# Seven block products in a second feed-forward, and modulation steps shared with ScalarE and GpSimd

## The chip, the cores and the metric

The kernel runs on one core of one Trainium2 chip. The metric is device time in microseconds of one execution, as the median of a few runs. The engines go by short names in the profile: PE is TensorE's matmul queue (PEld its weight loads), DVE is VectorE, ACT is ScalarE, POOL is GpSimd, and SP is the queue that issues nearly all DMAs.

## What is computed

Two layers of a transformer block on 256 image tokens (x) and 256 context tokens (ctx) of 1024 channels. Each layer has a feed-forward, a token mix (attention and pooling) and a second feed-forward. Ahead of each stands a norm with a shift and a scale, behind each a gate; these nine vectors per layer come from one conditioning vector per stream, which is the *modulation*.

```python
def mod_vectors(cvec, w_mod, b_mod):
    m = jax.nn.silu(cvec) @ w_mod + b_mod
    return jnp.split(m, N_MOD, axis=-1)

def sandwich_ffn(x, w_gate_up, w_down, g_pre, g_post, shift, scale, gate):
    h = modulate(rms_norm(x, g_pre), shift, scale)
    return x + 0.5 * gate * rms_norm(swiglu(h, w_gate_up, w_down), g_post)

for l in range(DEPTH):
    x = sandwich_ffn(x, ...); ctx = sandwich_ffn(ctx, ...)
    out_x, out_c = token_mix(...)
    x = sandwich_ffn(x + ..., ...)
    if not last: ctx = sandwich_ffn(ctx + ..., ...)
```

All inputs are float32. D_FF is 2816, so there are 22 blocks of 128 hidden channels, each with a gate and an up half. The last feed-forward of the second layer has only x.

## The kernel before

**Precision.** A float32 matmul is made of three faster ones. Every operand is split into a high part, which ScalarE rounds (`split`, line 570), and a low part, the difference, which VectorE subtracts. `mm3` (565) multiplies high by high, high by low and low by high. So each weight that is loaded costs ScalarE one rounding and VectorE one subtraction of two SBUF tensors before TensorE can use it.

**A feed-forward** (`ffn`, 930). For each of the 22 blocks: load the weights, split them (`Stream.prep`, 480, one block ahead), multiply the gate and up halves for all 512 tokens into two PSUM banks (names pg and pu), take silu and product, split again (g). After a group of blocks the down projection of that group follows (name pd), and its result is added up in y. The first blocks (START or LEAD, 2 or 3) are done for half of the tokens at a time, so that TensorE can begin while the other half is still being normed. With the last down projections the tokens are *closed* one tile of 128 after the other (`close`, 860): squares, the power -0.5 on GpSimd (`power`, 744, name rs_st), gate, residual, norm for the next stage, transposes on TensorE (pt), shift and scale, and the split into the next stage's input h.

**Seven products.** For the pair in `SEVEN`, here only the second layer's first feed-forward (1, 0), a block is not computed as eight products of quarter size but as seven, in Strassen's manner (`gate_up_seven`, 974; name p_ps): 84 matmuls of 256 columns instead of 48 of 512. For this GpSimd forms sums of the weights (`prep_seven`, 493; name s_wk), four additions of 128x512 per block, and once per feed-forward sums of the tokens (`Input.add_up`, 778), eight more, all of which are split as well. VectorE adds the partial products. The groups are then five of four to six blocks (`S_GROUPS`) instead of three (`F_GROUPS`). The tokens must be laid out in pairs, in the order 2, 0, 3, 1; the stage before has to close them in that order (`NEXT_SEVEN`, `ORDER`, `PAIRED`).

**Modulation** (`mod_steps`, 669). One vector takes nine steps. Eight load 512 KB of w_mod each (name wm) and multiply it by one scalar per partition, adding into an accumulator (acc) of 128x1024 for each of the two streams: a `tensor_scalar` for the first, a `scalar_tensor_tensor` for the others, both on VectorE. From the gate of the second layer's token mix on there is only one stream. The ninth step folds the accumulators: sixteen DMAs of 64 KB, three GpSimd additions per stream (part), a small matmul (pm). The first two vectors of layer 0 are made in another way at the start; the other sixteen, 144 steps, are a queue `todo`. After each block of a feed-forward `fill(rate)` (715) records so many steps of it: `RATE` in the first feed-forward (0, 0), 2.6 steps per block, `LATER` in (0, 1), 2.6, 4.2 and 5.6 in its groups, `NONE` in (1, 0).

**The order of the work.** Nothing is issued as it is written. `Recorder` takes every operation with a rank (its place in the program) and a price by engine and size (`price`, 216; a GpSimd addition is 0.155 us plus 2.09 ns per element of a partition, and each engine is priced for itself). `Recorder.order` (301) then plays the program through: at each step it takes the operation that can start first, by data, by its engine's clock and by a free place, and among equals the one of lowest rank. A `margin` lets an operation count as ready that much later, a `haste` earlier. The result is one fixed order per engine, which the chip follows with semaphores. All lines of the profile are therefore L384, where the operations are issued, and groups are told apart by the names of the tiles. Tiles live in numbered places: sixteen "big" ones for weights, h, g and y, ten "wk" ones of 4 KB per partition for wm, acc, part, tt, the sums and the closings, two for raw weights, eight PSUM banks.

Of the kernel before, what the change touches and what calls it, by code (L numbers as in the profile page):

```python
# [28 lines left out]
S_GROUPS = ((0, 4), (4, 8), (8, 12), (12, 16), (16, 22))  # L29
SEVEN = {(1, 0)}  # L30
NEXT_SEVEN = {(1, 0)}
ORDER = (2, 0, 3, 1)
# [7 lines left out]
LIMITS = {"ps": 1}  # L40
RATE = (2.6, 2.6, 2.6)
LATER = (2.6, 4.2, 5.6)
NONE = (0.0,) * 5
# [141 lines left out]
class Recorder:  # L185
# [9 lines left out]
    def __init__(self, places, limits):  # L195
        self.places, self.limits = places, limits
        self.ops = []
        self.seq = {}
        self.delay = 0
        self.margin = 0.0  # L200
        self.haste = 0.0
        for e in self.ENGINES:
            setattr(self, e, _Engine(self, e))
# [35 lines left out]
    def record(self, engine, method, args, kw):  # L239
# [16 lines left out]
        for v, target in [(v, False) for v in ins] + [(v, True) for v in outs]:  # L256
# [19 lines left out]
            keep.append((op, p0, p1, bits, writes))  # L276
            buf.log = keep
        op.after = after
        op.waits = len(after)
# [122 lines left out]
def tile_dit_block(  # L402
# [56 lines left out]
    class Stream:  # L459
        def __init__(self):  # L460
            self.plan = []
            self.ready = []
            self.raws = []
            self.taken = 0
            self.ahead = AHEAD
            self.sevens = 0

# [25 lines left out]
        def prep_seven(self, raw):  # L493

            (a11, a12), (a21, a22) = ((raw[:, i, 0:512], raw[:, i, 512:D]) for i in range(2))
            s12, s34 = wtile([P, 2, 512], "s12"), wtile([P, 2, 512], "s34")
            rec.margin = 0.0 if self.sevens else 2 * MARGIN
            self.sevens += 1
            nc.gpsimd.tensor_add(s12[:, 0, :], a21, a22)
            rec.margin = 0.0  # L500
            nc.gpsimd.tensor_sub(s12[:, 1, :], s12[:, 0, :], a11)
# [140 lines left out]
    def first_mod(j):  # L642
# [24 lines left out]
        rec.haste = 0.0  # L667

    def mod_steps(l, j):
        acc = [None, None]  # L670
        streams = (0,) if l == DEPTH - 1 and j >= 5 else (0, 1)
        for k in range(KD):
            def step(k=k):
                wm = wtile([P, D], "wm")
                nc.sync.dma_start(out=wm, in_=wmod[l, j, k])
                for v in streams:
                    if k == 0:
                        acc[v] = wtile([P, D], "acc")
                        nc.vector.tensor_scalar(
                            out=acc[v], in0=wm, scalar1=csil[:, k, v : v + 1], scalar2=None, op0=ALU.mult  # L680
                        )
                    else:
                        nc.vector.scalar_tensor_tensor(
                            out=acc[v], in0=wm, scalar=csil[:, k, v : v + 1], in1=acc[v], op0=ALU.mult, op1=ALU.add
                        )
# [26 lines left out]

    debt = [0.0]

    def fill(n):
# [40 lines left out]
    class Input:  # L756
# [3 lines left out]
        def __init__(self, paired):  # L760
# [5 lines left out]
            self.full = {}  # L766
            self.sums = None

        def __getitem__(self, b):
# [8 lines left out]
        def add_up(self):  # L778
# [3 lines left out]
            for o in range(2):  # L782
                one, two = self.full[ORDER[o]], self.full[ORDER[2 + o]]
                rec.margin = MARGIN
                a, b, c, d = one[:, lower, :], two[:, lower, :], two[:, upper, :], one[:, upper, :]
                nc.gpsimd.tensor_sub(a, b, a)
                rec.margin = 0.0
                nc.gpsimd.tensor_sub(b, c, b)
# [7 lines left out]
    def new_h(paired=False):  # L796
        return Input(paired)
# [13 lines left out]
    def normed(t, l, jshift, n, hf, Hn, sq):  # L811
# [16 lines left out]
        if Hn.paired:  # L828
            Hn.full[t] = hf

    def first_unit(t):
# [252 lines left out]
    def token_mix(l, nxt):  # L1084
# [249 lines left out]

        toks = (2, 3, 0, 1) if full else (0, 1)
        load_gate(l, 5, (0, 1) if full else (0,))
# [13 lines left out]
        for t in toks:  # L1350
# [4 lines left out]
            if Hn is None:  # L1355
                Hn = new_h()
            close(t, pd[t], None, False, nxt, Hn)
# [22 lines left out]

    ffn(0, 0, True, (0, 3), RATE, START, (CS, XS))
    token_mix(0, (0, 6))
    ffn(0, 1, True, (1, 0), LATER, LEAD, (CS, XS))
    ffn(1, 0, True, (1, 3), NONE, LEAD, (0, 1))
    token_mix(1, (1, 6))
# [107 lines left out]
```

## Time and profile before

| | us |
|---|---|
| median of 3 runs | 1662.52 |
| lowest and highest | 1661.26, 1665.65 |
| the profiled execution's own time | 1662.74 |
| its span, from the first to the last instruction | 1661.0 |
| TensorE busy in the span | 1615.6 |
| VectorE, ScalarE, GpSimd busy | 1211.8, 736.4, 355.7 |

By the timeline the first feed-forward begins about 40 us into the span and ends about 412, the first token mix ends about 604, the second feed-forward goes to about 980, the third to about 1334, the second token mix and the last feed-forward to the end. A group of the profile gives line, engine, operation, tiles written and read, shapes, the count, the busy time, the mean of one in ns, and the idle time of the engine ahead of it with what ended it. "Releaser" is inferred from semaphores. Buffer numbers are left out of the names, so w_big is any weight in a big place.

### The profile page before, as it was taken

Reading aid. Unit: us, or ns where it says so; the run is one execution under the profiler, and the core shown is the slowest. Engines: PE = TensorE matmul, PEld = TensorE weight load, DVE = VectorE, ACT = ScalarE, POOL = GpSimd, SP = SyncE. Lnnn points to the kernel's source line nnn. Section 1 sums busy time; section 2 is a strip of 40 time slices with the busy share of each in tenths; the row PEclk is TensorE's granted clock in tenths of the full one; section 3 lists DMA queues with packets and bytes.
Section 4 is the critical chain, followed back from the end, with each engine's and each line's share of the span. In section 5 each row is a group of like instructions: output and inputs, shape, how many; then the busy total and the mean of one; then the engine's idle time right before and its main releaser. Section 6 shows DMA issues by size and latency. Waiting matters only on the chain.

```text
span 1661.0 us, 23503 instructions
## 1 busy us (share of the span) xinstructions
PE 1615.6 (97%) x9074; PEld 1392.5 (84%) x9074; DVE 1211.8 (73%) x1662; ACT 736.4 (44%) x1292; POOL 355.7 (21%) x348
## 2 busy tenths in 40 slices
PE   6999999999999999999999989999999999899998
PEld 5988888888888788888888879989989888779997
DVE  7995766546789779867786588677788688975554
ACT  7522322225566563222222364434434567774442
POOL 1022011101132311110211045363454122210000
PEclk9999999999999999999999999999999999999999
DMA  9466556522221435666698413223233422355551
GB/s 376 185 229 247 203 193 224 183 108 83 89 75 65 160 115 212 237 202 229 217 344 306 150 47 106 77 102 128 77 108 122 143 77 82 128 202 194 201 196 58
DMA packets 98958, 269.09 MB, mean 162 GB/s; under 512 B 9424, under 2 KB 39328, under 8 KB 87072
## 3 DMA queue, kind: packets, MB, share of 16 engines
q1 hardware_dynamic: 98848, 267.60, 45.6%
q8 instruction: 71, 1.16, 0.3%
q14 instruction: 39, 0.32, 0.1%
HBM read 251.80 MB, written 1.09 MB: 152 GB/s over the span
## 4 chain that ended last, share of the span: by engine, by line
PE 85%; DVE 6%; ACT 5%; POOL 2%; issue 1%; DMA 1%; SPq 0%; DVEq 0%; POOLq 0%; ACTq 0%
PE pd_ps L384 26%; PE pg_ps L384 19%; PE pu_ps L384 19%; PE p_ps L384 11%; PE pv_ps L384 2%; PE pk_ps L384 2%; ACT n_wk L384 2%; POOL rs_st L384 2%; PE pq_ps L384 1%; DVE w_big L384 1%; DMA w_big<-in_wmod_dram 1%; PE pt_ps L384 1%; PE po_ps L384 1%; PE pp_ps L384 1%; ACT sx_wk L384 1%
## 5 line engine op out<-in xcount | busy, mean ns | idle before, releaser
L384 DVE TENSOR_TENSOR w_big<-raw_raw,w_big 128x1024 fp32r<-128x1024 f32 x293 | 371.2, 1282 | 124.1 <-ACT w_big L384 123.6
L384 PE MATMUL pd_ps<-w_big,g_big 128*128 128x512 f32 x1848 | 431.5, 394 | 0.0
L384 PEld LDWEIGHTS pd_ps<-w_big,g_big 128*128 128x128 f32 x1848 | 345.8, 188 | 78.4 <-ACT grows L384 0.2
L384 ACT ACTIVATE w_big<-raw_raw 128x1024 fp32r<-128x1024 f32 x293 | 302.8, 1053 | 231.7 <-DMA raw_raw<-in_wgu_dram 103.6
L384 PE MATMUL pu_ps<-h_big,w_big 128*128 128x512 f32 (+1 forms) x1944 | 366.5, 341 | 0.0
L384 PEld LDWEIGHTS pu_ps<-h_big,w_big 128*128 128x128 f32 x1944 | 303.7, 188 | 42.3
L384 PE MATMUL pg_ps<-h_big,w_big 128*128 128x512 f32 (+1 forms) x1752 | 331.8, 344 | 3.8 <-DVE h_big L384 2.4
L384 PEld LDWEIGHTS pg_ps<-h_big,w_big 128*128 128x128 f32 x1752 | 277.1, 191 | 44.1 <-DVE h_big L384 2.9
L384 DVE SCALAR_TENSOR_TENSOR acc_wk<-wm_wk,csil,acc_wk 128x1024 f32<-128x1024 f32 x196 | 245.2, 1290 | 78.8 <-DMA wm_wk<-in_wmod_dram 78.5
L384 POOL TENSOR_TENSOR part_wk<-part_wk 128x512 f32<-128x512 f32 (+2 forms) x84 | 89.0, 1060 | 495.6 <-DMA part_wk<-acc_wk 466.6
L384 ACT ACTIVATE g_big<-tt_wk 128x512 fp32r<-128x512 f32 (+1 forms) x84 | 49.2, 586 | 273.2 <-DVE tt_wk L384 257.2
L384 POOL TENSOR_SCALAR rs_st<-sq_st 128x1 f32<-128x1 f32 x24 | 7.6, 316 | 448.0 <-ACT n_wk L384 447.9
L384 POOL TENSOR_TENSOR s_wk<-raw_raw 128x512 f32<-128x512 f32 x38 | 63.8, 1687 | 131.6 <-DMA raw_raw<-in_wgu_dram 94.2
L384 PE MATMUL p_ps<-h_big,w_big 128*128 128x256 f32 x684 | 86.9, 281 | 0.0
L384 PEld LDWEIGHTS p_ps<-h_big,w_big 128*128 128x128 f32 x684 | 83.7, 189 | 0.3
L384 PE MATMUL p_ps<-ht_big,w_big 128*128 128x256 f32 x684 | 83.3, 280 | 0.0
L384 PEld LDWEIGHTS p_ps<-ht_big,w_big 128*128 128x128 f32 x684 | 81.6, 189 | 0.0
L384 DVE TENSOR_TENSOR g_big<-tt_wk,g_big 128x512 fp32r<-128x512 f32 (+1 forms) x84 | 57.8, 688 | 29.9 <-ACT g_big L384 29.9
L384 PE MATMUL pd_ps<-w_big,mix_big 128*128 128x512 f32 x288 | 71.9, 399 | 0.5 <-DVE mix_big L384 0.5
L384 ACT ACTIVATE tt_wk<-pg_ps 128x512 f32<-128x512 f32 (+1 forms) x67 | 35.8, 534 | 75.3 <-PE pg_ps L384 62.4
L384 DVE TENSOR_TENSOR y_big<-y_big,pd_ps 128x512 f32<-128x512 f32 x72 | 47.9, 683 | 27.9 <-PE pd_ps L384 27.8
L384 DVE TENSOR_TENSOR w_big<-s_wk,w_big 128x1024 fp32r<-128x1024 f32 x38 | 55.8, 1468 | 16.5 <-ACT w_big L384 16.4
(157 smaller groups left out, 1769.6 us busy)
## 6 DMA issues: line engine op xcount, KB each, us to landing
raw_raw<-in_wgu_dram SPq DMA_DIRECT2D x84, 1024.0 KB, 4.9
wm_wk<-in_wmod_dram SPq DMA_DIRECT2D x128, 512.0 KB, 6.9
raw_raw<-in_wdn_dram SPq DMA_DIRECT2D x44, 1024.0 KB, 5.2
part_wk<-acc_wk SPq DMA_DIRECT2D x224, 64.0 KB, 2.4
raw_raw<-in_wkq_dram SPq DMA_DIRECT2D x8, 1024.0 KB, 4.8
raw_raw<-in_wout_dram SPq DMA_DIRECT2D x8, 1024.0 KB, 4.9
w_big<-in_wmod_dram SPq DMA_DIRECT2D x7, 1024.0 KB, 15.0
gb_wk<-grow SPq DMA_DIRECT2D x10, 512.0 KB, 7.1
```

The lines of the kernel that those rows point to most:

```text
L384: getattr(getattr(nc, op.engine), op.method)(*[self.real(a) for a in op.args], **{k: self.real(a) for k, a in op.kw.items()})
```

## The change

- `SEVEN` gets (0, 1) as well: the first layer's second feed-forward, the second of four, uses seven products in its blocks 3 to 21, five groups, and halves by paired tokens.
- For this the first token mix closes its tokens in the order 2, 0, 3, 1 and keeps their normed values for the token sums.
- The steps of the modulation are spread anew: 3.6, 4.4 and 4.8 per block in the first feed-forward (93 in place of 57), 1.2 in the second, 1.3 in the third.
- While the first feed-forward is recorded (`helps`), the second stream of a step is made by a ScalarE product into a tile of its own ("pr", a wk place) and a GpSimd addition of 128x1024; the first of a vector is written into the accumulator directly. Afterwards both streams are VectorE's again.
- The margins of 6 and 12 us ahead of the first GpSimd sums are replaced by `hold`: in the planner's order, the first weight sum of each block and the first token sum come after the last operation of the last closing (`Input.done`).

```diff
-SEVEN = {(1, 0)}
-NEXT_SEVEN = {(1, 0)}
+SEVEN = {(0, 1), (1, 0)}
+NEXT_SEVEN = {(0, 6), (1, 0)}
...
-RATE = (2.6, 2.6, 2.6)
-LATER = (2.6, 4.2, 5.6)
+RATE = (3.6, 4.4, 4.8)
+LATER = (1.2,) * 5
+LAST = (1.3,) * 5
...
+        if self.hold is not None:
+            after.setdefault(self.hold, False)
         op.after = after
...
-            rec.margin = 0.0 if self.sevens else 2 * MARGIN
-            self.sevens += 1
+            rec.hold = H["now"].done
             nc.gpsimd.tensor_add(s12[:, 0, :], a21, a22)
-            rec.margin = 0.0
+            rec.hold = None
...
+                    c = csil[:, k, v : v + 1]
                     if k == 0:
                         acc[v] = wtile([P, D], "acc")
-                        nc.vector.tensor_scalar(
-                            out=acc[v], in0=wm, scalar1=csil[:, k, v : v + 1], scalar2=None, op0=ALU.mult
-                        )
+                    if v and helps[0]:
+                        o = acc[v] if k == 0 else wtile([P, D], "pr")
+                        nc.scalar.activation(o, wm, AF.Copy, scale=c)
+                        if k:
+                            nc.gpsimd.tensor_add(acc[v], acc[v], o)
+                    elif k == 0:
+                        nc.vector.tensor_scalar(out=acc[v], in0=wm, scalar1=c, scalar2=None, op0=ALU.mult)
                     else:
                         nc.vector.scalar_tensor_tensor(
-                            out=acc[v], in0=wm, scalar=csil[:, k, v : v + 1], in1=acc[v], op0=ALU.mult, op1=ALU.add
+                            out=acc[v], in0=wm, scalar=c, in1=acc[v], op0=ALU.mult, op1=ALU.add
                         )
...
-                rec.margin = MARGIN
+                rec.hold = self.done
                 a, b, c, d = one[:, lower, :], two[:, lower, :], two[:, upper, :], one[:, upper, :]
                 nc.gpsimd.tensor_sub(a, b, a)
-                rec.margin = 0.0
+                rec.hold = None
...
             Hn.full[t] = hf
+            Hn.done = rec.ops[-1]
...
-        toks = (2, 3, 0, 1) if full else (0, 1)
+        paired = nxt in NEXT_SEVEN
+        toks = (ORDER if paired else (2, 3, 0, 1)) if full else (0, 1)
...
-                Hn = new_h()
+                Hn = new_h(paired)
...
     ffn(0, 0, True, (0, 3), RATE, START, (CS, XS))
+    helps[0] = False
     token_mix(0, (0, 6))
-    ffn(0, 1, True, (1, 0), LATER, LEAD, (CS, XS))
-    ffn(1, 0, True, (1, 3), NONE, LEAD, (0, 1))
+    ffn(0, 1, True, (1, 0), LATER, LEAD, (0, 1))
+    ffn(1, 0, True, (1, 3), LAST, LEAD, (0, 1))
```

More of the change, by code (lines that the diff above doesn't have):

```diff
@@ L199, in __init__ @@
         self.delay = 0
+        self.hold = None
         self.margin = 0.0
@@ L465, in __init__ @@
             self.ahead = AHEAD
-            self.sevens = 0
         def add(self, src, parts, seven=False):
@@ L667, in first_mod @@
         rec.haste = 0.0
+    helps = [False]
     def mod_steps(l, j):
@@ L713, in tile_dit_block @@
     debt = [0.0]
+    helps[0] = True
     def fill(n):
@@ L767, in __init__ @@
             self.sums = None
+            self.done = None
         def __getitem__(self, b):
```

## The prediction

> **What bounds the kernel now.** I read the page first, for the share of each engine and the chain that ended last.
>
> ```profile
> span 1661.0 us, 23503 instructions
> PE 1615.6 (97%) x9074; PEld 1392.5 (84%) x9074; DVE 1211.8 (73%) x1662; ACT 736.4 (44%) x1292; POOL 355.7 (21%) x348
> PE 85%; DVE 6%; ACT 5%; POOL 2%; issue 1%; DMA 1%; SPq 0%; DVEq 0%; POOLq 0%; ACTq 0%
> ```
>
> TensorE (PE) is busy 97% of the span and makes 85% of the chain. An edit pays here if it takes matmuls away, and costs if it makes TensorE wait. So the next view is the table by stretches, cut at the stages that the edit touches: the first feed-forward (40 to 394), the second (613 to 944), the handover to the third (961 to 1022) and the third, which already uses seven block products (1022 to 1299). Columns: length, then busy time and instructions of PE, PEld, DVE, ACT and POOL, granted clock, DMA share, GB/s.
>
> ```profile
> 40.00:394.00 354.00, 354.00 (x1643) 293.04 (x1642) 240.72 (x256) 108.23 (x148) 38.68 (x38) 1.00 0.56 195
> 613.00:944.00 331.00, 330.98 (x1571) 275.13 (x1570) 252.06 (x254) 93.23 (x122) 51.60 (x48) 1.00 0.67 238
> 961.00:1022.00 61.00, 56.15 (x394) 51.96 (x394) 54.35 (x72) 39.41 (x81) 28.67 (x28) 0.97 0.11 38
> 1022.00:1299.00 277.00, 277.00 (x1982) 260.17 (x1981) 211.20 (x228) 116.30 (x153) 126.73 (x72) 1.00 0.31 108
> ```
>
> In all three feed-forwards TensorE has no gap, at full clock: DVE, ACT and POOL hide behind it completely. 4.85 us are idle in the handover. Nothing in these stages can be gained but matmul time; everything else is a question of whether the cover still holds.
>
> **The change part by part.** *Seven products.* The chain in order of time (start, length, what, count) has a plain block of the second feed-forward and the third feed-forward's groups of four blocks.
>
> ```profile
> 898.99 5.55 PE pg_ps L384 x24
> 904.54 5.52 PE pu_ps L384 x24
> ...
> 1054.14 39.60 PE p_ps L384 x336
> 1093.74 22.26 PE pd_ps L384 x96
> 1116.00 39.37 PE p_ps L384 x336
> 1155.37 22.17 PE pd_ps L384 x96
> 1177.54 39.70 PE p_ps L384 x336
> ```
>
> A plain block takes 5.55 + 5.52 = 11.07 us. Four seven-product blocks take 39.60, 39.37 and 39.70, so one takes 118.67 / 12 = 9.89. The first three blocks (LEAD) stay plain halves in both forms, so 19 blocks save 1.18 each: **22.4 us** off the path. The down projections have the same matmuls in five groups instead of three: nothing on TensorE; the extra accumulations on DVE lie under 22 us of TensorE per group.
>
> The groups of DVE in the first feed-forward, 40 to 394, before (count, busy us, mean ns, idle), price its operations:
>
> ```profile
> L384 DVE SCALAR_TENSOR_TENSOR acc_wk<-wm_wk,csil,acc_wk 128x1024 f32<-128x1024 f32 x88 | 110.0, 1289 | 26.7 <-DMA wm_wk<-in_wmod_dram 26.7
> L384 DVE TENSOR_TENSOR w_big<-raw_raw,w_big 128x1024 fp32r<-128x1024 f32 x68 | 84.0, 1255 | 34.7 <-ACT w_big L384 34.7
> L384 DVE TENSOR_TENSOR g_big<-tt_wk,g_big 128x512 fp32r<-128x512 f32 x22 | 15.4, 702 | 7.9 <-ACT g_big L384 7.9
> ...
> L384 DVE TENSOR_SCALAR acc_wk<-wm_wk,csil 128x1024 f32<-128x1024 f32 x14 | 10.1, 749 | 15.2 <-DMA wm_wk<-in_wmod_dram 15.2
> ```
>
> *What the second feed-forward needs from DVE.* In the third one, without modulation, DVE is busy 211.20 of 277. LATER puts 1.2 steps behind each block there, 26 in all, about 16 with two streams. A two-stream step averages (2 x 7 x 1.29 + 2 x 0.75) / 9 = 2.2 us, from these rows, a one-stream step half: 35 + 11 = 46 us, together 257 of 277, 93%. It fits as an average, but within a group of four blocks DVE runs behind and must recover under the 22 us down projection. I book **2 us** of TensorE waiting, with 0 and 15 as ends. LAST gives the third feed-forward 25 one-stream steps, 27 us: 238 of 277, hidden.
>
> *What moves into the first feed-forward.* RATE goes from 57 steps to 92: ten whole vectors and two steps, 82 products per stream, of which 11 start an accumulator, so 71 second-stream additions of 128x1024 go to POOL and 82 products to ACT. The groups of POOL and one of ACT in the same stretch:
>
> ```profile
> L384 POOL TENSOR_TENSOR part_wk<-part_wk 128x512 f32<-128x512 f32 x12 | 18.1, 1507 | 226.7 <-DMA part_wk<-acc_wk 226.2 <-issue 0.4
> L384 POOL TENSOR_TENSOR part_wk<-part_wk 128x256 f32<-128x256 f32 x12 | 10.6, 881 | 0.9
> L384 POOL TENSOR_TENSOR part_wk<-part_wk 128x128 f32<-128x128 f32 x12 | 8.8, 732 | 0.9
> ```
>
> ```profile
> L384 ACT ACTIVATE w_big<-raw_raw 128x1024 fp32r<-128x1024 f32 x68 | 70.1, 1053 | 81.4 <-DMA raw_raw<-in_wgu_dram 41.9 <-PE pd_ps L384 18.1 <-DMA raw_raw<-in_wdn_dram 8.9
> ```
>
> ACT: 82 x 1.05 = 86 us on top of 108, of 354: hidden. DVE: one stream less, 82 instead of 102 operations, so about 25 us less. DMA: 31 more 512 KB loads and four more vectors of sixteen 64 KB pieces are some 20 MB, 56 GB/s on 195, a share of about 0.72; the trace carried 0.95 without a TensorE gap:
>
> ```profile
> 831.00:876.00 45.00, 45.00 (x198) 36.63 (x197) 35.86 (x36) 11.28 (x12) 6.25 (x5) 1.00 0.95 329
> ```
>
> The waits that are new: a POOL addition waits for ACT's product, and an ACT product waits for a free wk place, which a POOL addition gives back. Behind it on ACT stand the roundings of the next weights, and behind a late addition on POOL the rs_st powers of the closings, for which TensorE's transposes wait. So the price hangs on POOL. No 128x1024 addition is in the trace. In the timelines of POOL and of DVE alone:
>
> ```profile
> 489.00 1.17 POOL L384 TENSOR_TENSOR dd_wk<-U_wk 128x591 f32<-128x591 f32 x1 [5.04 <-ACT U_wk L384]
> 490.25 1.17 POOL L384 TENSOR_TENSOR dd_wk<-dd_wk 128x589 f32<-128x589 f32 x1
> 491.49 2.86 POOL L384 TENSOR_TENSOR dd_wk<-dd_wk,U_wk 128x256 f32<-128x256 f32 x4
> ```
>
> ```profile
> 1091.87 2.28 POOL L384 TENSOR_TENSOR s_wk<-s_wk,raw_raw 128x512 f32<-128x512 f32 x1
> ...
> 1103.65 1.29 POOL L384 TENSOR_TENSOR s_wk<-raw_raw 128x512 f32<-128x512 f32 x1
> ```
>
> ```profile
> 1087.82 1.23 DVE L384 TENSOR_TENSOR w_big<-raw_raw,w_big 128x1024 fp32r<-128x1024 f32 x1 [0.40 <-ACT w_big L384]
> ...
> 1090.68 2.31 DVE L384 TENSOR_TENSOR w_big<-raw_raw,w_big 128x1024 fp32r<-128x1024 f32 x1
> ...
> 1102.88 1.39 DVE L384 TENSOR_TENSOR y_big<-y_big,pd_ps 128x512 f32<-128x512 f32 x2 [0.34 <-PE pd_ps L384]
> ```
>
> Alone, a 512-wide addition takes 1.29 us, a 256-wide one 2.86 / 4 = 0.72, a 591-wide one 1.17. So 1024 costs between 1024/591 x 1.17 = 2.0 and 1.29 + 2 x 0.57 = 2.4. And they are not alone: the addition that overlaps DVE's weight subtraction takes 2.28 instead of 1.29, and the subtraction 2.31 instead of 1.23. Each waited out the other. The accumulation that reads PSUM (two in 1.39) disturbed nobody, and the addition beside it took 1.29. So DVE's operations on two SBUF tensors and POOL's additions go one after the other, and the two engines' queues must fit into one stretch of time. A DVE operation holds POOL up for 2.28 - 1.29 = 1.0 us, a 512-wide addition holds DVE up for 1.1, some 0.2 less than it lasts; so 1.8 to 2.2 for 1024.
>
> The common stretch, of 354 us: weight subtractions 68 x 1.0 = 68, g 22 x 0.5 = 11, first stream 71 x 1.0 + 11 x 0.55 = 77, partition sums 20 x (1.1 + 0.5 + 0.3) = 38, additions 71 x 1.8 to 2.2 = 128 to 156. Total 322 to 350, 91 to 99%; before, with 88 + 14 accumulations and 12 sums, 68 + 11 + 96 + 23 = 198, 56%. The planner's prices know POOL and DVE singly and not this, so its order has no room for it. I take the middle, 336, and 92% of the time in use where both queue: 365, **11 us** over the 354. Ends: 0 (the low price, packed) and 43 (350 at 88%).
>
> *The hold.* It replaces a margin by a true predecessor in the planner's order: block sums on POOL come behind the last closing. Before, they ran into it. DVE in the handover, POOL's group of such sums on the page, one of them in the handover, then TensorE:
>
> ```profile
> 973.93 1.50 DVE L384 TENSOR_SCALAR n_wk<-x,rs_st 128x512 f32<-128x512 f32 x1 [0.45 <-POOL rs_st L384]
> ...
> 980.15 3.45 DVE L384 TENSOR_TENSOR h_big<-yg_wk,h_big 128x512 fp32r<-128x512 f32 x2
> ```
>
> ```profile
> L384 POOL TENSOR_TENSOR s_wk<-raw_raw 128x512 f32<-128x512 f32 x38 | 63.8, 1687 | 131.6 <-DMA raw_raw<-in_wgu_dram 94.2 <-DVE c_wk L384 30.4 <-DVE w_big L384 6.6
> ```
>
> ```profile
> 973.87 1.27 POOL L384 TENSOR_TENSOR s_wk<-raw_raw 128x512 f32<-128x512 f32 x1
> ```
>
> ```profile
> 983.66 4.51 PE L384 MATMUL pg_ps<-h_big,w_big 128*128 128x256 f32 x23 [2.42 <-DVE h_big L384]
> ```
>
> Two subtractions of 512 took 3.45, and TensorE waited 2.42 for them. That wait goes: **-2.5 us** of the 4.85. What is late next is the sums themselves, four additions and eight for the tokens, 12 x 1.69 = 20 us behind the last closing; the three lead blocks give 3 x 11.07 = 33 us of cover. Ends: -4.85 and +3. The handover into the second feed-forward gets the same twelve additions anew: **+1**, ends 0 and +4; the other token order there moves no matmul.
>
> **The sum**, against the profiled execution's own 1662.74 us (the span of 1661.0 and 1.7 around it; the median of the three is 1662.52): 1662.7 - 22.4 + 2 + 11 - 2.5 + 1 = 1651.8, so **1652**.
>
> **The rivals.** *POOL and DVE saturate (slower).* With the high price and less than perfect order, the common stretch doesn't fit and the first feed-forward is stretched. ACT stands at a product without a place, the weights behind it are late, and the backlog ends in front of rs_st in the closings. At 350 us and 88% that is 43 us: 1662.7 - 22.4 + 2 + 43 - 2.5 + 1 = 1684. It decides from 21 us on, that is where the common stretch with its gaps exceeds 375. For it: 2.28 and 2.31. Against it: the third feed-forward shows both engines queueing with no gap in TensorE, and the last steps may slip behind the closings. The Trainium skill, SBUF — State Buffer, section "SBUF: two separate sides", has it as a rule: the pair of ports that VectorE and GpSimd share is an exclusive lock, held by one instruction to its end; the rows above agree, 2.28 for 1.29. The Trainium skill, GPSIMD Engine Reference, section "Elementwise — side-by-side cycle accounting", gives 4497 ns for an addition of 2048; half of it, 2.25 as an estimate, would make the sum 71 x 2.05 + 194 = 340.
>
> *DVE is the bound in the second feed-forward.* For a seven-product group at 93% of DVE on average, a backlog of a few us per group on the two-stream part would give 15 us instead of 2: with the rest as forecast 1665, no change. Against it: nothing waited at 76%.
>
> *All is hidden.* The steps fit in (low price): 0 and 0 for the 11 and the 2 and the full 4.85 of the handover give 1662.7 - 22.4 - 4.9 + 1 = 1636.
>
> **How the numbers follow.** 0.3% is 5 us, about what a measurement of this kernel tells from no change. Faster, from the whole gain to a stretch of some 16 us: 0.50. Within 5 us, the forecast's own high end or DVE late in the second feed-forward: 0.15. Slower, by saturation: 0.35. The range leaves out the last us of the hidden case and the worst of saturation: 1637 to 1690; the likeliest case's own is 1637 to 1657.
>
> **What would show it.** Right: the p_ps groups with twice their matmuls, 9.9 us a block; pg_ps and pu_ps fewer; POOL additions of 128x1024 about 71, their mean well over 2.4 (2.8 to 3.4) because they wait for DVE; DVE's acc operations in the first stage likewise; TensorE's gap of 2.42 behind h_big gone. Wrong: TensorE idle over 25 us in the first feed-forward, with ACT waiting for POOL or TensorE waiting for w_big; gaps in TensorE between blocks in the second one with DVE as releaser; an addition near 1.3 us, or additions that leave DVE alone.

## The result and the profile after

| | before | after |
|---|---|---|
| median, us | 1663.47 (1661.26 to 1665.65, 4 runs) | 1769.24 (1768.11 to 1770.55, 4 runs) |
| ratio, 95% interval | | 1.0641, 1.0625 to 1.0657 |
| span of the profiled execution, us | 1661.0 | 1766.3 |

The change makes the kernel 6.4% slower; forecast was 1652, in a range of 1637 to 1690. The page of after, its first line on the span, the engines' busy time, the clock row of the forty slices and the shares of the chain that ended last:

```profile
span 1766.3 us, 25533 instructions
PE 1624.5 (92%) x9758; PEld 1427.7 (81%) x9758; DVE 1395.3 (79%) x1718; ACT 861.6 (49%) x1439; POOL 735.0 (42%) x503
PEclk9988998899799999999999999999999999999999
PE 42%; DVE 23%; DMA 10%; ACT 7%; issue 7%; SPq 6%; POOL 5%; POOLq 0%; DVEq 0%; ACTq 0%
```

TensorE's share of the chain fell from 85% to 42%, VectorE's rose from 6% to 23%. The clock row shows the place: the five values of 8 and 7 lie in the third to the eleventh slice of 44 us each, all in the first feed-forward. The table by stretches, here cut at the first matmul of each stage, before and after (length, busy time and count of PE, PEld, DVE, ACT, POOL, clock, DMA share, GB/s; the first and the second feed-forward of each):

```profile
37.00:412.00 375.00, 374.68 (x1739) 309.89 (x1740) 258.82 (x290) 125.14 (x191) 45.60 (x51) 1.00 0.54 188
604.00:981.00 377.00, 375.46 (x1802) 311.94 (x1800) 282.02 (x305) 118.42 (x181) 63.89 (x67) 1.00 0.62 219
```

```profile
36.00:518.00 482.00, 400.30 (x1756) 325.75 (x1757) 373.82 (x276) 212.69 (x275) 291.20 (x146) 0.90 0.55 190
712.00:1085.00 373.00, 355.43 (x2455) 328.84 (x2455) 316.21 (x347) 157.32 (x241) 179.94 (x116) 0.98 0.39 135
```

The first feed-forward takes 107 us more: TensorE stands idle for 81, and nearly the same matmuls take 400.3 instead of 374.7, at a granted clock of 0.90. In the second one the chain has pieces of seven-product matmuls (start, length, what, count):

```profile
987.39 37.00 PE p_ps L388 x312
```

It takes 3 us less, not the 19 of the forecast (-22.4 + 2 + 1): its matmul time did fall by 19 (374.9 to 355.8 between its first matmul and the next stage's; the rows above are cut at whole us), but 16 us of it came back as idle time. The largest wait there:

```profile
PE pd_ps L388 <- ACT g_big L388: 10.9, 2, 6.4
```

Behind both of these waits stands VectorE: ScalarE rounds a product (g) that VectorE had added up late, because weight subtractions and accumulations ahead of it were stretched beside GpSimd's sums of weights. An accumulation of this stage takes 1526 ns in the mean, 1292 before. The third feed-forward is 1 us shorter. From the first matmul of a stage to the first of the next, as used for every run below, that is 374.6 to 481.7, 376.4 to 373.3 and 353.7 to 352.7, and TensorE's idle time in them 0.2 to 81.3, 1.5 to 17.6 and 3.8 to 2.2.

What TensorE waited for in the first feed-forward of after (total us, times, longest; the largest):

```profile
PE pm_ps L388 <- DMA part_wk<-acc_wk: 32.7, 3, 13.5
PE pm_ps L388 <- POOL part_wk L388: 22.2, 3, 15.7
PE pr_ps L388 <- DVE col L388: 21.1, 3, 8.1
PE pd_ps L388 <- DVE tt_wk L388: 1.7, 1, 1.7
```

These are not the weights. pm is the small matmul that folds a finished vector, pr the transpose of a gate's row: 76 of the 81 us. Nobody needs either at once, but TensorE takes its instructions in order, and the planner had put them 6 us (MARGIN) behind the time at which it believed their data to be there. One such place in TensorE's timeline (start, length, count, idle time before):

```profile
147.50 13.45 PE L388 MATMUL pd_ps<-w_big,g_big 128*128 128x512 f32 x57
171.30 0.59 PE L388 MATMUL pm_ps<-sel,part_wk 128*128 128x8 f32 x2 [10.35 <-DMA part_wk<-acc_wk]
171.74 13.82 PE L388 MATMUL pd_ps<-w_big,g_big 128*128 128x512 f32 x48
```

Why the vector was late, the groups of VectorE and of GpSimd in this stage say (count, busy us, mean ns, idle before):

```profile
L388 DVE SCALAR_TENSOR_TENSOR acc_wk<-wm_wk,csil,acc_wk 128x1024 f32<-128x1024 f32 x71 | 158.6, 2234 | 54.9 <-DMA wm_wk<-in_wmod_dram 53.6 <-DVE acc_wk L388 0.4
L388 DVE TENSOR_TENSOR w_big<-raw_raw,w_big 128x1024 fp32r<-128x1024 f32 x68 | 127.4, 1892 | 10.8 <-ACT w_big L388 10.8
L388 DVE TENSOR_TENSOR g_big<-tt_wk,g_big 128x512 fp32r<-128x512 f32 x22 | 30.7, 1396 | 5.2 <-ACT g_big L388 5.1
L388 DVE TENSOR_TENSOR tt_wk<-tt_wk,pu_ps 128x512 f32<-128x512 f32 x22 | 14.9, 677 | 0.8 <-ACT tt_wk L388 0.8
```

```profile
L388 POOL TENSOR_TENSOR acc_wk<-acc_wk,pr_wk 128x1024 f32<-128x1024 f32 x71 | 218.6, 3079 | 73.3 <-ACT pr_wk L388 60.7 <-PE pu_ps L388 9.6
```

Against before, an accumulation takes 2234 ns for 1289, a weight subtraction 1892 for 1255, a g subtraction 1396 for 702. The product that reads PSUM (tt_wk, 677) is untouched. An addition that was not held up and one accumulation that met an addition, in the timelines of the two engines:

```profile
85.16 2.40 POOL L388 TENSOR_TENSOR acc_wk<-acc_wk,pr_wk 128x1024 f32<-128x1024 f32 x1 [9.62 <-PE pu_ps L388]
```

```profile
66.43 3.44 DVE L388 SCALAR_TENSOR_TENSOR acc_wk<-wm_wk,csil,acc_wk 128x1024 f32<-128x1024 f32 x1
```

The addition costs 2.40 us when nothing holds it up, the upper end of what was estimated, and VectorE's operation beside one takes 3.44 instead of 1.28. That the two wait for each other is called "the turns" below.

### The profile page after: what moved, and what is told of

The parts are those of the page before. It is cut to its first block, busy times and chain, and to the rows that moved or that the text cites. A ratio compares the mean times of both kernels' runs of the same rounds, so it can differ in the third digit from the quotient of the medians.

```text
span 1766.3 us, 25533 instructions
## 1 busy us (share of the span) xinstructions
PE 1624.5 (92%) x9758; PEld 1427.7 (81%) x9758; DVE 1395.3 (79%) x1718; ACT 861.6 (49%) x1439; POOL 735.0 (42%) x503
## 4 chain that ended last, share of the span: by engine, by line
PE 42%; DVE 23%; DMA 10%; ACT 7%; issue 7%; SPq 6%; POOL 5%; POOLq 0%; DVEq 0%; ACTq 0%
PE pd_ps L388 14%; PE p_ps L388 10%; DVE w_big L388 7%; DMA wm_wk<-in_wmod_dram 6%; SPq L388 6%; PE pg_ps L388 5%; DVE acc_wk L388 5%; PE pu_ps L388 5%; POOL s_wk L388 2%; ACT n_wk L388 2%; PE pk_ps L388 2%; PE pv_ps L388 2%; POOL rs_st L388 2%; DMA raw_raw<-in_wgu_dram 1%; PE pq_ps L388 1%
## 5 line engine op out<-in xcount | busy, mean ns | idle before, releaser
L388 PEld LDWEIGHTS pd_ps<-w_big,g_big 128*128 128x128 f32 x1848 | 355.8, 194 | 101.0 <-ACT g_big L388 11.8
L388 PE MATMUL pu_ps<-h_big,w_big 128*128 128x256 f32 (+1 forms) x1488 | 260.0, 327 | 0.0
L388 POOL TENSOR_TENSOR acc_wk<-acc_wk,pr_wk 128x1024 f32<-128x1024 f32 x71 | 218.6, 3079 | 73.3 <-ACT pr_wk L388 60.7
L388 PEld LDWEIGHTS pu_ps<-h_big,w_big 128*128 128x128 f32 x1488 | 220.4, 190 | 23.9
L388 PE MATMUL pg_ps<-h_big,w_big 128*128 128x256 f32 (+1 forms) x1296 | 227.7, 330 | 1.4 <-ACT h_big L388 1.4
L388 PEld LDWEIGHTS pg_ps<-h_big,w_big 128*128 128x128 f32 x1296 | 195.5, 193 | 24.0 <-ACT h_big L388 1.8
L388 PE MATMUL p_ps<-h_big,w_big 128*128 128x256 f32 x1368 | 174.6, 281 | 0.0
L388 PE MATMUL p_ps<-ht_big,w_big 128*128 128x256 f32 x1368 | 169.4, 281 | 1.2 <-DVE w_big L388 1.2
L388 PEld LDWEIGHTS p_ps<-h_big,w_big 128*128 128x128 f32 x1368 | 167.8, 189 | 0.7
L388 PEld LDWEIGHTS p_ps<-ht_big,w_big 128*128 128x128 f32 x1368 | 165.0, 189 | 1.6 <-DVE w_big L388 1.4
L388 ACT ACTIVATE pr_wk<-wm_wk,csil 128x1024 f32<-128x1024 f32 x71 | 80.8, 1148 | 126.7 <-DMA wm_wk<-in_wmod_dram 104.8
```

The source lines that it names most:

```text
L388: getattr(getattr(nc, op.engine), op.method)(*[self.real(a) for a in op.args], **{k: self.real(a) for k, a in op.kw.items()})
```

## The experiments

Diffs are against the changed kernel ("after") or the kernel before, as said. "Stage" is the length from the stage's first matmul to the next one's.

**Is it the turns, or the work that was moved?** Two runs keep the change's rates and take the additions away. *VectorE alone*, against after:

```diff
-    helps[0] = True
+    helps[0] = False
```

> The changed kernel with both streams of every step on VectorE; the steps stay where the change puts them (92 in the first feed-forward). Theory A (GpSimd's additions and VectorE's operations on two SBUF tensors take turns, and their sum doesn't fit): without the additions VectorE has about 330 us of own work in the 354 us up to the first closing, so the first feed-forward is back at 372 to 390 us and the time at 1640 to 1665. Rival B (92 steps are too many for the loads, the wk places or the folds, whichever engine adds): still above 1720.

*Memsets for the additions*, against after. This leaves out the second stream's sums over eleven vectors; GpSimd is kept as long, by operations that read nothing:

```diff
-                            nc.gpsimd.tensor_add(acc[v], acc[v], o)
+                            nc.gpsimd.memset(o, 0.0)
+                            nc.gpsimd.memset(acc[v], 0.0)
+                            nc.gpsimd.memset(acc[v][:, 0:512], 0.0)
```

> The changed kernel with each of the 71 second-stream additions replaced by three GpSimd memsets (two of 1024, one of 512), about as long as one addition alone, that read nothing; it leaves out the second stream's sums over the first feed-forward. ScalarE's products, their places and the chain behind them stay. Theory A: memsets don't take turns with VectorE, so the first feed-forward is 372 to 395 us and the time 1640 to 1670. Rival C (GpSimd's own time, or ScalarE waiting in its queue for products and places, whatever GpSimd reads): 1740 to 1770 as in the changed kernel.

With VectorE alone 1680.3 (1675.8 to 1683.2; ratio to before 1.0094, 1.0072 to 1.0116), the first stage 397.9 with 15.3 us idle. With memsets 1676.5 in one run, the stage 388.0, idle 9.1. The second one's groups of GpSimd and VectorE:

```profile
L388 POOL MEMSET acc_wk<- 128x1024 f32 x71 | 67.9, 956 | 6.6 <-ACT acc_wk L388 3.6
L388 POOL MEMSET pr_wk<- 128x1024 f32 x71 | 67.5, 956 | 43.6 <-ACT pr_wk L388 39.6 <-DMA part_wk<-acc_wk 3.5
L388 POOL MEMSET acc_wk<- 128x512 f32 x71 | 37.9, 533 | 2.6
```

```profile
L388 DVE SCALAR_TENSOR_TENSOR acc_wk<-wm_wk,csil,acc_wk 128x1024 f32<-128x1024 f32 x71 | 93.6, 1318 | 55.2 <-DMA wm_wk<-in_wmod_dram 54.5
L388 DVE TENSOR_TENSOR w_big<-raw_raw,w_big 128x1024 fp32r<-128x1024 f32 x68 | 83.9, 1244 | 29.0 <-ACT w_big L388 28.9
```

956 + 956 + 533 ns is 2.45 us, as long as an addition alone; the loads, ScalarE's products, the folds and GpSimd's busy time per step are those of the change. VectorE's operations are back at 1318 and 1244, and 94 of the 107 us are gone. So the turns of the two engines on SBUF operands cost this time, not GpSimd's queue. And the 71 second-stream accumulations are cheaper on VectorE itself than shared: 84 us. The sizes that theory A expected were partly missed: with VectorE alone the stage is 8 us above its range, and both wholes lie above theirs, by 15 and 7 us; the second feed-forward idles 15 and 18 us in them. Over its 374.6 the first stage keeps 23 us with VectorE alone and 13 with memsets, which no run takes apart.

**Is it the place of the fold?** The margin ahead of the fold matmul and of the row's transpose, 40 us instead of 6, against after:

```diff
-            rec.margin = MARGIN
+            rec.margin = 40.0
...
-                rec.margin = MARGIN
+                rec.margin = 40.0
```

> The changed kernel with the margin ahead of the folding matmul and of the gate rows' transpose raised from 6 to 40 us in the planner, so that they stand later in TensorE's queue. Rival D (the stretch comes only from TensorE standing at the fold, which could wait): TensorE's waits at pm and pr, about 100 us, go and the time is 1650 to 1680. Theory A: the work that takes turns is still too long, the waits come back at other places (weights, g, the closings) and the time stays at 1715 or more.

1761.6 in one run, the stage 474.4 with 73.6 us idle. The waits of TensorE there:

```profile
PE pd_ps L388 <- ACT tt_wk L388: 23.6, 4, 10.0
PE pd_ps L388 <- ACT y_big L388: 11.5, 1, 11.5
PE pd_ps L388 <- DVE g_big L388: 8.2, 2, 4.1
```

No wait of pm or pr is among the stage's waits any more, and 7 us were gained: the fold was where the lateness showed, not its cause.

**What of the second feed-forward?** *Seven products alone*, against after, the modulation on VectorE only and mostly left in the second and third stage:

```diff
-RATE = (3.6, 4.4, 4.8)
-LATER = (1.2,) * 5
-LAST = (1.3,) * 5
+RATE = (2.6, 2.6, 2.6)
+LATER = (2.4,) * 5
+LAST = (1.6,) * 5
...
-    helps[0] = True
+    helps[0] = False
```

> The changed kernel with both streams on VectorE and before's 2.6 steps per block in the first feed-forward; the rest goes to the second (2.4 per block) and the third (1.6). Theory A: the first feed-forward is as before (372 us), the third hides its 35 steps, and in the second VectorE is asked for more than its time in the two-stream part: seven products gain 22 us and some 5 to 15 are given back there, 1645 to 1660. Rival E (seven products bring nothing in the second feed-forward, because VectorE bounds it anyway): 1663 or more.

*The second stage bare*, the same with RATE 3.7, LATER 0 and LAST 2.9:

> The changed kernel with VectorE alone on the modulation (no ScalarE products, no GpSimd additions), 3.7 steps a block in the first feed-forward, none in the second and 2.9 a block in the third: the second feed-forward has its 19 seven-product blocks and no modulation beside them. Theory (the modulation left there, 46 us of VectorE, eats the 22 us that the products save): the second feed-forward takes 354 to 358 with at most 3 us of TensorE idle, 19 less than in the changed kernel. Rival (seven products in a feed-forward of two parts stall by themselves, in the weights' loads and roundings): 365 or more, with the same idle time. The first and third stages may be longer for what they took over; the whole is not what this run is for.

Seven products alone, where 1645 to 1660 was expected: 1728.1 (1725.6 to 1730.4), ratio 1.039 (1.0374 to 1.0405); first stage 374.6 as before, second 428.2 with 54.3 us idle. Bare: the whole 1718.0 in one run, since the third stage took 415.6, but the second 350.1 with 2.3 us idle. TensorE's largest waits in the second stage of the former, then the row of that stage in the latter:

```profile
PE p_ps L388 <- DVE w_big L388: 23.6, 7, 6.6
PE pd_ps L388 <- DVE g_big L388: 9.2, 4, 3.3
PE pd_ps L388 <- ACT g_big L388: 4.9, 3, 2.6
```

```profile
621.00:971.00 350.00, 347.71 (x2446) 324.82 (x2444) 272.44 (x304) 160.78 (x240) 154.03 (x100) 1.00 0.29 100
```

Without modulation beside it the stage saves 26.3 us: its matmul time falls by 27, of it some 23 in the block products and 2 in the folds that left with the modulation. With 2.4 steps a block it loses 52, with 1.2 it gains 3. VectorE's room is what seven products use up; with 2.4 steps TensorE then waits for w_big, the weights it subtracts.

**Does sharing fit at all, if less is shared?** The kernel before with `helps` in its first feed-forward, at its own rate of 2.6: 44 additions.

> The kernel before with the sharing alone: in the first feed-forward the second stream's products go to ScalarE and its sums to GpSimd, at the old rate of 2.6 steps a block (44 additions of 128x1024 instead of 71); seven products, order holds and the later rates as before. The time before on this chip is about 1663. Theory A (the two queues take turns, and it costs where their sum no longer fits): weight subtractions 73, g 16, partition sums 26, first stream 51, additions 44 x 2.3 = 101, together 267 of 354, 75 %, against 82 % that the whole change reached when it was stretched: the first feed-forward takes 375 to 390 at most and the whole 1660 to 1685. Rival (every addition delays the chain by its own, however full the stretch is): 107 x 44 / 71 = 66 us, the first feed-forward at 440 and the whole at about 1730.

The same with the folds 40 us late:

> The kernel before with the sharing alone at 2.6 steps a block, as in the run sharing alone (first feed-forward 416.7 us, 42 more than before), but with a margin of 40 us instead of 6 ahead of the fold matmul and of the transpose of a gate's row. Theory (at 75 % of the common stretch the two queues fit, and TensorE lost its 35 us of idle time by standing, in its own order, at matmuls of the modulation that came late): the first feed-forward takes 375 to 390. Rival (the turns delay weights and products themselves, wherever the fold stands): 405 to 420, with the waits moved to pd_ps and pg_ps, as with 71 additions.

Sharing alone is 1704.2 (1703.2 to 1705.8), ratio 1.0244 (1.0226 to 1.0263), the stage 416.7, idle 35.0; with late folds 1707.7 in one run, the stage 411.0, idle 28.6. My theory expected at most 390 in both. The rival came closer, but at 42 us for 44 additions not by its proportion of 66. So sharing costs where the sum of the turns has room, too. The next two runs ask why. The planner was told of them, first in this kernel, then in after:

```diff
+        near = [v for v in ins if isinstance(v, View) and v.buf.tag != "ps" and int(np.prod(v.shape[1:])) >= 128]
+        op.turns = method != "memset" and (engine == "gpsimd" and bool(near) or engine == "vector" and len(near) > 1)
...
-                    t = max(clock[e], ready[op], at)
+                    t = max(clock[e], ready[op], at, port if op.turns else 0.0)
...
+                if op.turns:
+                    port = op.end
```

> The sharing alone at 2.6 steps a block with 44 additions (first feed-forward 416.7 us as it stood), and the planner told of the turns. Theory O (order): 375 to 390, TensorE idle under 10 us. Rival P (places): 400 or more, with VectorE waiting for loads of wm_wk as before (55 us in 17 waits).

> The changed kernel, and the planner is told of the turns: an operation of VectorE on two SBUF tensors and an addition of GpSimd are never placed over one another; rates and everything else as in the change. Theory O (the order was wrong because it did not know the turns; the stretch itself fits badly but nearly): the first feed-forward falls from 482 to 400 to 430. Rival P (places: a product holds a work place until it is added, the loads of the modulation come late whatever the order): 450 or more. Third, neither: the sum of 377 us is simply too much at any order above some 85 %, which would leave 440 to 450.

The rule leaves out VectorE's product with one SBUF tensor, the first of each vector, though this was held up as well: 1181 ns in the mean in the changed kernel, 749 before. And the rival, too few work places, in the kernel before with `"wk": 9` for 10:

> The kernel before with nine work places instead of ten, no sharing. Theory P (places are what is short): the first feed-forward gets 10 us or more longer than its 374.6, and other stages too. Theory O (order): it stays within 3 us.

With 44 additions the stage falls from 416.7 to 386.5 and its idle time from 35.0 to 6.9 (1670.1 in one run). TensorE's waits in that stage, as it stood and with the planner's knowledge:

```profile
PE pr_ps L388 <- DVE col L388: 27.5, 2, 22.5
PE pm_ps L388 <- DMA part_wk<-acc_wk: 6.3, 1, 6.3
```

```profile
PE pr_ps L393 <- DVE col L393: 4.7, 2, 3.3
PE pg_ps L393 <- DVE w_big L393: 2.1, 1, 2.1
```

The additions still take 2891 ns in the mean (2897 as it stood): the turns are as long, but what is due first now comes first. So 30 of the 42 us were the order. With nine places the first stage is 374.9, idle 0.1: without sharing, one place fewer does not matter there (the whole is 1672.4 in one run, lost in later stages). It does not test sharing, whose products hold a place of their own until they are added. With 71 additions the same knowledge brings only 19 of the 107 us, 462.6 with 68.4 idle (1743.0 in one run); TensorE's largest waits there are now for VectorE's w_big, 21.4 us at pg_ps and 19.6 at pd_ps. That lies in the places' range and above the 440 to 450 of the third theory. Whether the sum itself is too much there, or the places run short, no run separates; nor does one tell what the remaining 12 us with 44 additions are made of. In the second feed-forward of that run, where GpSimd's sums of weights take turns with VectorE as well, the knowledge did help: 363.5 with 10.1 idle, 373.3 with 17.6 before it, and an accumulation takes 1340 ns, not 1526.

**The hold, and the best use of both.** *The hold alone*, in the kernel before:

```diff
-                rec.margin = MARGIN
+                rec.hold = self.done
```

(and the same for the weight sums)

> The kernel before with only the hold in place of the two margins. The prediction's step: -2.5 us at the handover from the second to the third feed-forward, ends -4.85 and +3, so 1660.8 where the kernel before has 1663.3; the wait of 2.4 us for h_big goes and GpSimd's block sums come behind the closing. Rival: what is late next takes it all back, no change within 1 us, with a wait of the first seven-product matmuls for s_wk or w_big in its place.

1659.0 (1657.4 to 1661.7), ratio 0.9975 (0.9965 to 0.9985); the third stage 349.1 for 353.7. The handover in TensorE's and VectorE's timelines:

```profile
981.41 2.97 PE L388 MATMUL pg_ps<-h_big,w_big 128*128 128x256 f32 x23
```

```profile
980.05 1.28 DVE L388 TENSOR_TENSOR h_big<-yg_wk,h_big 128x512 fp32r<-128x512 f32 x2
```

The two h subtractions take 1.28 us where before they took 3.45, since three of GpSimd's sums stand behind them now. The wait of 2.42 is gone, and the 23 matmuls behind it take 2.97 where they took 4.51: a gap's cost is the gap and a slow stretch behind it. (In the changed kernel's timeline above, too: 57 matmuls in 13.45 ahead of the gap of 10.35, 48 in 13.82 behind it.)

*Seven products from block 12 on* in the second stage, VectorE alone, the hold. In the first form (3.0 steps a block in the first stage, 3.4 and 1.2 in the second, 1.2 in the third) the plain blocks 3 to 11 run in halves; in the second they are whole again, for which h is laid out in another way, and the modulation is packed ahead (4.2, then 0; 1.3); the third form starts at block 8.

```diff
+FROM = {(0, 1): 12, (1, 0): 3}
...
-                if seven:
+                if seven and f >= FROM[l, ff]:
```

> The changed kernel with VectorE alone on the modulation, and the second feed-forward's seven products from block 12 on instead of block 3 (10 blocks, not 19); rates 3.0 a block in the first, 3.4 in the second's plain blocks and 1.2 in its seven-product ones, 1.2 in the third. Theory (seven products pay as far as VectorE has room beside them): 10 x 1.18 = 11.8 us saved, some 2 to 5 given back, no gaps in the first feed-forward: 1652 to 1658 where the kernel before has 1663. Rival (VectorE is late wherever it does seven products and modulation, even at 1.2 steps): the second feed-forward idles 10 us or more and the whole is 1663 or above.

> VectorE alone on the modulation, the hold, seven products in the second feed-forward from block 12 on (10 blocks), the plain blocks 3 to 11 there 512 wide again instead of in halves, and the modulation packed ahead of the seven-product blocks: 3.0 steps a block in the first feed-forward, 4.2 in the plain blocks of the second, none in its seven-product ones, 1.3 in the third. In the run with seven products from block 12 a plain block in halves took 12.15 us and a whole one 11.07 before, 9 x 1.08 = 10 us, and the stage idled 8.7 us. Theory (seven products pay where VectorE carries no modulation beside them): second feed-forward 364 to 368, third 349 to 353, the whole 1648 to 1656 where the kernel before has 1663. Rival (4.2 two-stream steps a block are already too many beside plain blocks, or the third stage is late): 1660 or more.

> As the run before it, but seven products from block 8 on (14 blocks) and more modulation in the rest: 3.1 steps a block in the first feed-forward, 4.8 in the second's plain blocks, 0.6 in the four blocks after them, 1.6 in the third. Four more blocks save 4 x 1.18 = 4.7 us. Theory (there is room for it): 2 to 5 us below the run before it. Rival (VectorE is full: 4.8 steps of 2.2 us beside some 6 us of other work fill a plain block's 16.7): 5 us or more above it, with TensorE waiting for w_big or g_big in the second feed-forward's first eight blocks or in the third.

*The planner's knowledge* with the hold alone, with the second form, and with less modulation in the third stage:

> The hold alone (1659.0 where the kernel before has 1662.9), and the planner told of the turns. Without sharing, both engines meet in the third feed-forward's block sums and in the partition sums only, and those stretches idle little: theory O gives 0 to -3 us beside the hold alone, the rival (a planner that spaces them apart delays the sums and so the weights) 0 to +4.

> Seven products in the second feed-forward from block 12 on, whole plain blocks, modulation of 3.0, 4.2, 0 and 1.3 steps a block (1662.2, even with the kernel before, as it stood), and the planner told of the turns. The hold with the turns stands at 1655.8 and differs from this in the modulation and the ten blocks. Theory O (order): the second feed-forward falls from 370 to 364 to 367, the third from 357 to 351 to 354, the first token mix by 5 as it did there: 1648 to 1653, below the hold with the turns. Rival (VectorE's room): second and third stay within 2 us of 370 and 357, and only the token mix gains: 1656 to 1659.

> The same with less modulation in the third feed-forward: 3.2, 4.6, 0 and 0.9 steps a block. If the third stage is long for its 28 steps (357 against 349 without any), 9 fewer give 2 to 3 us back there, and 4.6 instead of 4.2 beside the plain blocks costs less than that, since the stage's first twelve blocks have room (theory). Rival: the plain blocks are full at 4.2 and the second stage loses what the third gains, or more.

| kernel | median | ratio, 95% interval | 2nd stage (idle) | 3rd (idle) |
|---|---|---|---|---|
| hold alone | 1659.0 | 0.9975 (0.9965 to 0.9985) | 376.2 (1.5) | 349.1 (1.8) |
| from block 12, halves | 1665.5 | 1.0019 (1.0008 to 1.0030) | 376.9 (8.7) | 352.6 (2.6) |
| from block 12, whole | 1662.2 | 1.0003 (0.9994 to 1.0013) | 369.9 (6.1) | 357.2 (5.9) |
| from block 8, whole | 1680.3 | 1.0112 (1.0097 to 1.0127) | 382.7 (19.6) | 360.6 (7.5) |
| hold, turns known | **1655.8** | **0.9964** (0.9952 to 0.9976) | 376.2 (1.3) | 350.6 (1.8) |
| from 12, whole, turns known | 1665.9 | 1.0025 (1.0016 to 1.0034) | 379.4 (15.1) | 352.6 (2.4) |
| the same, less in the third | 1677.9 | 1.0095 (1.0081 to 1.0109) | 392.7 (23.5) | 350.6 (1.5) |

The first form's matmul time in its stage fell by 6.7 us (374.9 to 368.2) and its idle time rose by 7.2, so the whole is its rival's. That halves cost 1.1 us a block, as the next expectation has it, was a misreading: its 12.15 adds up the busy times of pg_ps and pu_ps, whose matmuls overlap, and with whole blocks the stage's matmul time fell by only 4.4 more in nine blocks, 0.5 a block at most. The second form saves 6.5 us in its stage and pays more for the 28 steps in the third, 357.2 where it is 349.1 without any; its whole is the rival's, too. So is the one from block 8 on, 18 us above. For the second form the planner's knowledge made the second stage worse, 370 to 379, and the third better, 357 to 353: neither theory nor rival. With 19 blocks it had made the second stage better, so which way it goes there hangs on the rest of the order. Moving 9 steps back from the third made the second 393, as that run's rival had it; I read this as VectorE having no more room there, which no run tests by itself. The fastest version on record is the hold with a planner that knows the turns, 0.4% below the kernel before. Beside the hold alone its stages gain most in the first token mix, 187.0 for 192.4, where I had not looked for it: TensorE's wait of 3.9 us for qa_wk there is gone. On the whole the two ratios' intervals overlap, so that it beats the hold alone is not shown.

## Why the prediction was wrong, point by point

- **Seven products, 22.4 us.** Right as matmul time: 84 matmuls a block in the chain's piece shown above are 9.96 us (9.89 forecast), the stage's busy time fell by 19, and the bare stage saved 26.3.
- **VectorE in the second feed-forward, 2 us.** Mis-sized: idle time rose by 16 (1.5 to 17.6), near the 15 that the rival with DVE as the bound had. That the work fits as an average, at 93%, did not keep the gaps to 2 us: the runs with 1.2 steps a block idle 10 to 18 there, the bare one 2. And the step priced an accumulation at the 1.29 us of a stage without GpSimd's sums; beside these it took 1.53.
- **The first feed-forward, +11 us.** This is the step that failed: "I take the middle, 336, and 92% of the time in use where both queue: 365". The mechanism was right, as the memsets showed, and so were the 71 additions and their mean (3079 ns, "2.8 to 3.4"; with the 11 first products they make 82 a stream, so 92 steps, not the 93 in the list of the change). Both sizes were wrong. The addition was at its upper price, 2.40 alone. With durations alone, less 0.1 to 0.2 us of each that does not hold, I estimate the turns at 377: accumulations 83, weights 72, other subtractions 16, additions 163, partition sums 43. That is over the 354 before any gap. And the two queues did not fill 92%: 377 of 482 is 78%, 81% with the planner's knowledge. (Without the 21 us of the stage that the 354 leave out, these are 82% and 85%.) The rival named the mechanism and stopped at 43 us, because it took 350 us at 88%. Neither it nor the forecast had TensorE's own queue: the fold matmuls and the row's transposes that stand there 6 us behind a planned time. It was the place of 76 us, yet moving them alone gave back 7. The loss of clock, 26 of the 107, was in no term.
- **What was to be hidden.** ScalarE went from 125 to 213 us of busy time (88, 86 forecast), and its share stayed out of the way; the DMA share was 0.55 over the longer stage.
- **The hold, -2.5.** Right in mechanism, too small: -3.9 for the whole alone, as the 2.42 of waiting took 1.5 of slower matmuls along. In the change the third stage gave most of it back to its 25 steps, 352.7 where it is 349.1 without. The **+1** at the handover before it: TensorE's waits for n_wk in the second stage rose from 1.5 to 3.6, so 2.
- **Against saturation** I had put that in the third feed-forward both engines queue without a gap. The runs show why this was no evidence: how much two queues can be filled hung on what was due and in which order, 30 us of it at 44 additions, not on one stage that happened to have slack.

The Trainium skill's rule that the prediction weighed, the exclusive lock in SBUF — State Buffer, section "SBUF: two separate sides", is what the first stage shows for operations on two SBUF tensors: 3.44 us for 1.28 beside an addition, 677 ns unchanged for the operation with a PSUM operand, and none of it beside memsets. The 2.25 for the addition, which the prediction estimated from the Trainium skill, GPSIMD Engine Reference, section "Elementwise — side-by-side cycle accounting", was measured as 2.40.

## What to carry to other kernels

Before work goes from VectorE to GpSimd, price it in the resource that both need: here an accumulation takes 1.28 us on VectorE and its addition 2.40 on GpSimd, so an idle engine made the common stretch longer. A quarter left empty was not enough: 267 us of turns in 354 cost 42 us, and still 12 with the better order. Give the planner the turns as a resource of its own before judging how much fits, and measure: one version got slower by it. Then look at what TensorE has in its own order behind late work: small matmuls that nobody needs stop it just as well.

## What the runs showed of the hardware

TensorE was slower behind its gaps. In the first feed-forward, with nearly the same matmuls, the granted clock and busy time went with the idle time: 1.00 and 374.7 us with 0.2 us idle, 0.98 and 379.9 with 6.9, 0.95 and 382.0 with 35, 0.93 and 394.6 with 68, 0.90 and 400.3 with 81. Each us of gaps cost about 0.2 to 0.3 more at the larger values. Two of the rows, with 44 additions in the planner's old order and in the new one:

```profile
38.00:455.00 417.00, 382.04 (x1741) 313.65 (x1742) 280.83 (x240) 178.52 (x242) 171.73 (x94) 0.95 0.50 169
```

```profile
37.00:424.00 387.00, 379.89 (x1740) 312.95 (x1741) 274.19 (x239) 177.83 (x242) 170.31 (x95) 0.98 0.54 183
```

A memset of GpSimd neither held up VectorE's operations on two SBUF tensors nor was held up by them, unlike an addition: in the run with memsets, accumulations that overlapped nothing of GpSimd's but memsets took 1.28 us (55 cases, 1.28 alone), weight subtractions 1.22 (37 cases, 1.22 alone), and no memset of 128x1024 took over 0.98. It did hold up VectorE's product with one SBUF tensor, 0.75 us alone: the two that met only memsets took 1.47 and 2.81 us.
